# Attention stage in a written order with planned weight steps, first gate tile joined to its fill

## The chip, the cores and the metric

The kernel runs on one core of a Trainium2 chip. The metric is the device time of one execution in microseconds; the time of a kernel is the median over its runs. The core has five engines with instruction queues of their own: TensorE (PE; its weight loads are listed apart as PEld), VectorE (DVE), ScalarE (ACT), GpSimd (POOL) and SyncE (SP), which here only issues DMA transfers. Each engine works through its own instructions in order and waits on semaphores for the others.

## The reference

One layer of a hybrid decoder, T = 1024 positions, width D = 1024, all in float32:

```python
h = rms_norm(x, norm_mix_pre)
q, k, v, cb, cc, cx, g_att, g_conv = split(h @ w_in)       # 6 parts of 512 columns, 2 of 1024
# stick-breaking attention, 8 heads of 64, strictly causal, t = query, s = key:
z = (q . k) / sqrt(64)
A[t, s] = sigmoid(z[t, s]) * prod(1 - sigmoid(z[t, j]) for s < j < t)
o = A @ v
y_att  = o @ w_att_branch
y_conv = (cb * causal_dwconv3(cc * cx)) @ w_conv_branch
m = sigmoid(g_att) * y_att + sigmoid(g_conv) * y_conv
x = x + rms_norm(m @ w_out, norm_mix_post)
h = rms_norm(x, norm_ffn_pre)
a, g = split(causal_dwconv3(h @ w_up))                     # 2 x 2816 columns
x = x + rms_norm((gelu(g) * a) @ w_down, norm_ffn_post)
```

## The kernel before

**Products.** A float32 factor is held as two fp16 halves, high and low, and a product is three passes of fp16 matmuls, `PASSES = ((0, 0), (0, 1), (1, 0))`. One 128 x 512 output of depth 1024 is thus 24 matmuls, and a projection tile of 128 columns for all 1024 positions 48.

**A weight tile and its scale.** Before a weight tile (128 x 1024, 512 KB) can be used it is fetched by a DMA that SyncE issues (`wfetch`), its squares are summed per partition on ScalarE (`sumsq`), and `scale_of` turns the sum into a power of two: VectorE casts the 128 partial sums to bf16 (`rb`, L69 to L71), TensorE adds them over the partitions with a matmul against ones (`pr`, L74), and three tiny VectorE operations on the bits of the sum give the scale and its inverse (L76 to L79). Then `split` writes the high half on ScalarE (L86) and the low half on VectorE (L87). `prep(name)` does this for weights in the order of the list `wseq`, some tiles ahead of the one that is asked for. The sums `pr` are numbered in that order; in the stage they share three PSUM banks (`pm`) with the outputs of the fill.

**The attention stage.** Heads are taken in four pairs j. For a pair, `units_of()` gives six units of up to 512 keys by two query tiles of 128, so there are 24 units and 48 query tiles; the tile `0_1_00` below is pair 0, p = 1, first key 0, second of the unit's two tiles. `stage1` handles one query tile: the scores `z` on TensorE (L455, and a mask matmul); two sigmoids on ScalarE, `R` (of -z, L464) and `be` (of z, L465); two scans along the keys on VectorE, one per head, which turn `R` into running products from right to left (L468); the weights `be` times the shifted `R` (L473); their high half by a ScalarE copy (L476) and low half by a VectorE subtraction (L477), both written over `R`; and a DMA transpose of both into `wT` that SyncE issues. `stage3` multiplies a unit's `wT` with v into `o` (L502), two units behind.

**The fill.** Between these pieces the kernel interleaves independent work for TensorE, as generators with one step per few matmuls: `v_tile` 4 to 7, for each pair `qk_tile` of the next pair's q and k and `conv_tile` (three projections `cc`, `cx`, `cb` and the gated convolution, result `pf`), then `p_split` (the scale of all four `pf` and their split to `p16`), and `branch(0, d)` for d = 0 to 7, the products of the convolution branch with the weights `wc0` to `wc3`, two d per weight. `merge` advances the fill in proportion to the attention's matmuls.

**What sets the order.** The kernel is written with the Tile framework. Its scheduler orders the instructions of each engine from the program order, dependences, priorities and its own model of durations. `stage1` and `stage3` run at high priority, and `stage3` is held behind a given matmul (`tc.issue_after`). So the written place of a fill step is not its place on an engine.

**Behind the stage.** `branches(0, 1, 2)` are the first three products `ywa` = o x `wa` (one weight for two of them). Then `blocks(q)` prepares sums and differences of blocks of `hT`, the normalised input in fp16 halves: the tiles `T1` to `T4` and the operand `hB` on VectorE (L601 and on). `gates(0)` computes the gate tile 0 (`gc0` and `ga0`, 48 matmuls each, sigmoids into two `xp` tiles), `pair_fetch`, `pair_sums` and `pair_split` prepare the weights of gate pair `g1`, and `merge_m(0)` forms the merged tile 0. The gate pairs `g1` to `g7` follow; their first products read `hB` and the split `g1` weights.

Of the kernel before, what the change touches and what calls it, by code (L numbers as in the profile page):

```python
# [24 lines left out]
P = 128  # L25
# [8 lines left out]
KH = KD // 2  # L34
PASSES = ((0, 0), (0, 1), (1, 0))


class Layer:
# [19 lines left out]
    def scale_of(self, sm, n, keep=False, slack=0):  # L58

        nc = self.nc  # L60
        if keep:
            r = self.const.tile([P, 4], F32, tag=f"sc{self.nsc}", name=f"sc{self.nsc}", bufs=1)
        else:
            r = self.smp.tile([P, 4], F32, tag="sc", name=f"sc{self.nsc}", bufs=16)
        self.nsc += 1
        rb = self.smp.tile([P, 1], BF16, tag="rb", name=f"rb{self.nsc}", bufs=8)
        if n > 1:
            nc.vector.tensor_reduce(r[:, 0:1], sm[:, 0:n], AX.X, ALU.add)
            nc.vector.tensor_copy(rb, r[:, 0:1])  # L69
        else:  # L70
            nc.vector.tensor_copy(rb, sm[:, 0:1])  # L71
        pool, shape, tag = self.sum_psum
        ps = pool.tile(shape, F32, tag=tag, name=f"pr{self.nsc}")
        nc.tensor.matmul(ps[:, 0:1], self.ones, rb, start=True, stop=True)  # L74
        ri = r.bitcast(I32)
# [85 lines left out]

    def rstd_of(self, src, name):
# [46 lines left out]
    def build(self):  # L209
# [8 lines left out]
        for j in range(4):  # L218
            if j < 3:
                nt("q", j + 1), nt("k", j + 1)  # L220
            nt("cc", j), nt("cx", j), nt("cb", j)
        for i in range(4):
# [3 lines left out]
        nt("gc", 0), nt("ga", 0)  # L226
# [44 lines left out]
    def mixer(self, mid):  # L271
        tc, nc, a = self.tc, self.nc, self.a
        hT = self.hp.tile([P, 2, KD, T], F16, tag="hT", name="hT")
        with ExitStack() as ph1:
# [74 lines left out]
            def qk_tile(j, which):  # L349
                w, inv = self.prep(f"{which}{j}")  # L350
# [17 lines left out]
                yield  # L368

            def conv_tile(j):  # L370
# [3 lines left out]
                for n, which in enumerate(("cc", "cx", "cb")):  # L374
                    w, inv = self.prep(f"{which}{j}")
# [65 lines left out]
            def stage1(u, tt, tl):  # L441
# [4 lines left out]
                nb = W // P  # L446
                z = pat.tile([P, 2, NH], F32, tag="z", name=f"z{nm}", bufs=2)
                for n, (hq, hk) in enumerate(PASSES):
                    for h in range(2):
                        d = ds(64 * h, 64)  # L450
                        m = nc.tensor.matmul(z[:, h, :W], s["q"][d, hq, ds(i * P, P)], s["k"][d, hk, ds(lo, W)],
                                             start=n == 0, stop=n == 2 and not u["top"], skip_group_check=True)
                if u["top"]:
                    for h in range(2):
                        m = nc.tensor.matmul(z[:, h, W - P:W], self.identb, self.maskb, start=False, stop=True,  # L455
                                             skip_group_check=True)
                u["last"] = m
                R = att.tile([P, 2, NH + 1], F32, tag="R", name=f"R{nm}", bufs=4)
                be = att.tile([P, 2, NH], F32, tag="be", name=f"be{nm}", bufs=2)
                if u["top"]:  # L460
# [3 lines left out]
                nc.scalar.activation(R[:, :, :W], z[:, :, :W], AF.Sigmoid, scale=s["cz"][1])  # L464
                nc.scalar.activation(be[:, :, :W], z[:, :, :W], AF.Sigmoid, scale=s["cz"][0])  # L465
# [4 lines left out]
                if not u["end"]:  # L470
                    carry[tl] = self.smp.tile([P, 2, 1], F32, tag="cy", name=f"cy{nm}", bufs=4)
                    nc.vector.tensor_copy(carry[tl], R[:, :, 0:1])
                nc.vector.tensor_tensor(be[:, :, :W], be[:, :, :W], R[:, :, 1:W + 1], ALU.mult)  # L473
                w = R.rearrange("p h s -> p (h s)").bitcast(F16)[:, :4 * W]
                wv = [w[:, ds(2 * W * hl, 2 * W)].rearrange("p (h s) -> p h s", h=2) for hl in range(2)]
                nc.scalar.activation(wv[0], be[:, :, :W], AF.Copy)  # L476
                nc.vector.tensor_tensor(wv[1], be[:, :, :W], wv[0], ALU.subtract)  # L477
                nc.sync.dma_start_transpose(u["wT"][:, ds(tl * 4 * u["nb"], 4 * nb), :], w)
# [4 lines left out]
            def stage3(u, after):  # L483
# [7 lines left out]
                with tc.issue_after(after):  # L491
                    for q, (hw, hv) in enumerate(((1, 0), (0, 0), (0, 1))):
                        for b in range(NB):
                            sb = lo // P + b
                            both = sb <= 2 * p
                            nb0 = min(NB, 2 * p + 1 - lo // P)
                            for h in range(2):
                                k0, k1 = (2 * hw + h) * nb0 + b, (2 * hw + h) * NB + b + 4 * NB
                                rhs = u["wT"][:, k0:k1 + 1:k1 - k0, :] if both else u["wT"][:, k1, :]
                                out = o[64 * h:64 * h + 64, n0:n0 + 2 * P] if both else \  # L500
                                    o[64 * h:64 * h + 64, n0 + P:n0 + 2 * P]
                                nc.tensor.matmul(out, v16[sb // 2][:, sb % 2, j, 1 + h if hv else 3 * h, :], rhs,  # L502
                                                 start=first and q == 0 and b == 0, stop=q == 2 and b == NB - 1,
                                                 skip_group_check=True)
# [10 lines left out]

            def attention():
                us = list(units_of())
                lag = 2
                for k in range(len(us) + lag):
                    if k < len(us):  # L520
                        u = us[k]
                        while "cz" not in stk.get(u["j"], {}):
                            yield 0
                        u["wT"] = att.tile([P, 32, P], F16, tag="wT", name=f"wT{u['nm']}", bufs=2)
                        for tl in (1, 0):
                            with tc.high_priority():
                                stage1(u, 2 * u["p"] + tl, tl)
                            yield u["nb"]
                    if k >= lag:
                        with tc.high_priority():  # L530
                            stage3(us[k - lag], us[min(k, len(us) - 1)]["last"].ins)
                        yield u["nb"] if k < len(us) else 4

            def chain(*gens):
                for g in gens:
                    yield from g

            def merge(main, n_main, fill, n_fill):

                done, seen, more = 0, 0, True  # L540
                for k in main:
                    seen += k
                    want = seen * n_fill // n_main if k else done + 1
                    while done < want and more:
                        more = next(fill, "end") != "end"
                        done += 1
                assert not more or next(fill, "end") == "end" or True
                for _ in fill:
                    pass

            for which in "qk":
                for _ in qk_tile(0, which):
                    pass
            gens = [v_tile(tt) for tt in range(4, 8)]
            for j in range(4):
                if j < 3:
                    gens += [qk_tile(j + 1, "q"), qk_tile(j + 1, "k")]
                gens.append(conv_tile(j))
            gens += [p_split()] + [branch(0, d, pm) for d in range(8)]
            merge(attention(), 4 * 3 * (2 + 4 + 2 + 4 + 4 + 4), chain(*gens), 32 + 3 * 34 + 4 * 49 + 1 + 64)  # L560

# [8 lines left out]
        with ExitStack() as ph2:  # L570
            sig = {}

            def gates(d):
                for bi, which in enumerate(("gc", "ga")):
                    w, inv = self.prep(f"{which}{d}")
                    sc = sgn[:, 8 + 8 * bi + d:9 + 8 * bi + d]
                    self.mul(sc, inv_h, inv)
                    s = self.xp.tile([P, T], F32, tag="x", name=f"s{which}{d}")
                    for c in range(2):
                        ps = pm.tile([P, NH], F32, tag="pm", name=f"p{which}{d}_{c}")  # L580
                        for _ in self.cm_half(w[0], hT, ps, c):
                            pass
                        nc.scalar.activation(s[:, ds(c * NH, NH)], ps, AF.Sigmoid, scale=sc)
                    sig[which, d] = s


# [47 lines left out]
            branches(0, 1, 2)  # L634
# [5 lines left out]
            gates(0)  # L640
# [7 lines left out]
            ms = [merge_m(0)]  # L648
# [483 lines left out]
```

## Time and profile before

| | |
|---|---|
| median of 3 runs | 1386.92 us (1383.72 to 1388.22) |
| the profiled execution | 1389.26 us |
| its span (first to last instruction) | 1387.5 us |
| mean granted clock of TensorE | 0.978 of full speed |
| busy: TensorE, VectorE, ScalarE, GpSimd | 94%, 72%, 58%, 3% of the span |

The span is divided roughly into the head (norm, first projections) up to 73 us, the attention stage up to 451 us, the gate pairs and the output projection, and the feed-forward network. A row of groups of the profile reads: line, engine, operation, output <- inputs by the program's names, shape, count | busy time in all in us, mean ns of one | idle time of the engine just before them and what ended it. A row of the timeline reads: start in us, length in us, engine, line, operation, names and shape, count, and in brackets the wait ahead of it in us and who ended it. A row of waits reads: who waited <- for whom: time in all, number of times, longest.

### The profile page before, as it was taken

What the parts mean: (1) busy time and instruction counts of PE and PEld (TensorE: products, weight loads), DVE (VectorE), ACT (ScalarE), POOL (GpSimd) and SP (SyncE); (2) the same over time, 40 slices, a digit from 0 to 9 for tenths busy, and PEclk for the clock granted to TensorE, in tenths of its full rate; (3) what the DMA queues carried; (4) which work ended last, traced back from release to release, by engine and by line L of the source; (5) the groups of instructions that cost most, each with busy time, mean ns of one, the idle gap of its engine ahead of it and who ended that gap; (6) DMA issues with size and microseconds to landing.
All of it is one profiled execution on the core that took longest, in us unless ns stands there. A gap on an engine that the chain in (4) does not pass through costs nothing. (4 is left out here: it accounts for less than half of the span.)

```text
span 1387.5 us, 17025 instructions
## 1 busy us (share of the span) xinstructions
PE 1299.4 (94%) x6543; PEld 598.0 (43%) x6543; DVE 1004.6 (72%) x1649; ACT 804.7 (58%) x1138; POOL 48.2 (3%) x69
## 2 busy tenths in 40 slices
PE   5998879888889999999999999999999999999997
PEld 3443434333434444444454444444444444444443
DVE  5669695857741797878688876963882893598848
ACT  6665655546536465775466576664765765576522
POOL 1000000000000000000110000010001001000001
PEclk9999999999999999999999999999999999999999
DMA  7235442534511001251341135156127318712115
GB/s 259 77 65 103 96 95 66 106 81 90 109 46 47 31 32 60 92 182 46 107 140 43 61 114 190 46 131 158 61 90 123 122 61 186 223 61 107 61 61 197
DMA packets 109394, 139.60 MB, mean 101 GB/s; under 512 B 79088, under 2 KB 79088, under 8 KB 109312
## 3 DMA queue, kind: packets, MB, share of 16 engines
q1 hardware_dynamic: 105360, 124.28, 29.6%
q0 software_dynamic: 3952, 14.23, 5.6%
q8 instruction: 51, 0.84, 0.2%
q14 instruction: 31, 0.25, 0.1%
HBM read 94.45 MB, written 25.17 MB: 86 GB/s over the span
## 5 line engine op out<-in xcount | busy, mean ns | idle before, releaser
L1002 PEld LDWEIGHTS <-wh_u 128*128 128x128 f16 x1848 | 178.7, 98 | 217.7 <-issue 4.0
L897 PE MATMUL pd<-wdh,f 128*128 128x512 f16 x1056 | 233.9, 383 | 10.2 <-DVE wdh L87 5.6
L897 PEld LDWEIGHTS <-f 128*128 128x128 f16 x1056 | 104.0, 99 | 138.5 <-issue 14.3
L76 DVE TENSOR_SCALAR sc<-pr 128x1 int32<-128x1 int32 x75 | 10.8, 152 | 110.0 <-PE pr L74 109.9
L1002 PEld LDWEIGHTS <-wh_g 128*128 128x128 f16 x588 | 56.8, 98 | 70.6 <-ACT wh_g L86 2.3
L712 PE MATMUL py<-wh_wo,m 128*128 128x512 f16 x384 | 83.9, 379 | 0.0
L901 ACT ACTIVATE y<-pd,sd 128x512 f32<-128x512 f32 x64 | 42.3, 693 | 63.2 <-PE pd L897 56.9
L87 DVE SCALAR_TENSOR_TENSOR wh_u<-ws_u,sc,wh_u 128x1024 f16<-128x1024 f32 (+1 forms) x66 | 72.1, 1100 | 8.9 <-ACT wh_u L86 8.9
L86 ACT ACTIVATE wh_u<-ws_u,sc 128x1024 f16<-128x1024 f32 (+1 forms) x66 | 64.2, 998 | 22.6 <-DVE ws_u L837 12.6
L476 ACT ACTIVATE R<-be 128x1024 f16<-128x1024 f32 (+3 forms) x48 | 39.2, 839 | 51.3 <-DVE be L473 39.4
L1079 DVE SCALAR_TENSOR_TENSOR ugu<-cgu,cw_g,ugu 128x1023 f32<-128x1023 f32 (+1 forms) x44 | 56.3, 1279 | 9.7 <-ACT ugu L1077 9.5
L203 PE MATMUL pq<-hT,wh_q 128*128 128x512 f16 x192 | 50.3, 422 | 13.1 <-DVE pf L394 11.0
L468 DVE TENSOR_TENSOR_SCAN R<-R,zero 128x256 f32<-128x256 f32 (+3 forms) x64 | 47.9, 804 | 16.1 <-ACT R L464 10.8
L1079 DVE SCALAR_TENSOR_TENSOR ua<-cau,cw_a,ua 128x1023 f32<-128x1023 f32 (+1 forms) x44 | 56.2, 1278 | 2.0 <-ACT ua L1077 1.8
L712 PEld LDWEIGHTS <-m 128*128 128x128 f16 x384 | 37.5, 98 | 44.1
L465 ACT ACTIVATE be<-z,cz 128x1024 f32<-128x1024 f32 (+3 forms) x48 | 42.4, 903 | 23.0 <-DVE R L477 14.5
L502 PE MATMUL o<-wT,v 128*64 128x256 f16 x480 | 31.0, 281 | 25.2 <-DVE o L511 12.7
L464 ACT ACTIVATE R<-z,cz 128x1024 f32<-128x1024 f32 (+3 forms) x48 | 41.7, 894 | 16.1 <-PE z L455 13.2
L203 PE MATMUL pk<-hT,wh_k 128*128 128x512 f16 x192 | 45.5, 395 | 4.6 <-DVE R L461 4.3
L307 PE MATMUL pv<-wh_v,hT 128*128 128x512 f16 x192 | 45.3, 392 | 3.1 <-ACT wh_v L86 1.7
L56 ACT ACTIVATE jk_u<-ws_u 128x1024 bf16<-128x1024 f32 x44 | 46.4, 1055 | 2.6 <-DMA ws_u<-w_up_nt 1.9
L203 PE MATMUL pcx<-hT,wh_cx 128*128 128x512 f16 x192 | 46.0, 388 | 0.0
(606 smaller groups left out, 2543.7 us busy)
## 6 DMA issues: line engine op xcount, KB each, us to landing
ws_u<-w_up_nt SPq DMA_DIRECT2D x44, 512.0 KB, 3.5
yd<-y POOLq DMA_DIRECT2D x24, 512.0 KB, 5.3
ds<-w_down SPq DMA_DIRECT2D x22, 512.0 KB, 6.2
wd<-w_down SPq DMA_DIRECT2D x22, 512.0 KB, 3.5
ws_g<-w_in_nt SPq DMA_DIRECT2D x14, 512.0 KB, 3.5
x<-x SPq DMA_DIRECT2D x8, 512.0 KB, 8.8
ws_wo<-w_out SPq DMA_DIRECT2D x8, 512.0 KB, 6.7
xr<-x SPq DMA_DIRECT2D x8, 512.0 KB, 4.0
```

What stands on the lines that cost most here:

```text
L56: self.nc.scalar.activation(self.junk(f"jk_{name}"), src, AF.Square, accum_out=acc)
L86: self.nc.scalar.activation(dst[:, 0, :], src, AF.Copy, scale=s)
L87: self.nc.vector.scalar_tensor_tensor(dst[:, 1, :], src, s, dst[:, 0, :], ALU.mult, ALU.subtract)
L203: nc.tensor.matmul(ps, w[:, wi, ds(k * P, P)], hT[:, hi, k, ds(c * NH, NH)], start=n == 0, stop=n == last)
L307: nc.tensor.matmul(pv, hT[:, hi, k, ds(tt * P, P)], wv[k // 2][:, wi, ds((k % 2) * NH, NH)], start=n == 0, stop=n == 3 * KD - 1)
L465: nc.scalar.activation(be[:, :, :W], z[:, :, :W], AF.Sigmoid, scale=s["cz"][0])
L468: nc.vector.tensor_tensor_scan(rev, rev, self.zero.broadcast_to([P, W]), 2.0 ** 14 if u["top"] else carry[tl][:, h, :], ALU.mult, ALU.add)
L712: nc.tensor.matmul(ps, m16[k][:, hi, ds(tt * P, P)], wo[k][:, wi, sl], start=k == 0 and p == 0, stop=k == 7 and p == 2)
L897: nc.tensor.matmul(ps, f16[g][k][:, hi, ds(tt * P, P)], w[k][:, wi, sl], start=n == 0, stop=n == 3 * GROUPS[g] - 1)
L901: nc.scalar.activation(y[:, sl], ps, AF.Copy, scale=sm[:, 0:1])
L1002: nc.tensor.matmul(ps, w[wt][:, wi, ds(wc * NH + k * P, P)], self.block(i, hi, k), start=first and n == 0, stop=n == 3 * KH - 1, skip_grou ...
L1079: nc.vector.scalar_tensor_tensor(u[:, lag:], c[:, :T - lag], sm[:, 2 - lag:3 - lag], u[:, lag:], ALU.mult, ALU.add)
```

## The change

It is one change in four parts.

1. **Written order.** From `qk_tile(0)` to the end of `attention()` the program runs under `tc.manual_schedule` for TensorE, ScalarE, VectorE and SyncE: on these engines each instruction keeps the place that it has in the program. GpSimd is still placed by the scheduler. `high_priority` and `issue_after` go.
2. **One query tile at a time.** `stage1` is cut into `scores` (TensorE and the two sigmoids), `scan`, `weigh`, and `turn` in two parts (the ScalarE copy; the VectorE subtraction and the transpose). The loop over tiles takes them in the order: scores of this tile, copy of the last tile, scans of this tile, subtraction and transpose of the last tile, weigh of this tile; after a unit's second tile the products of the unit two back; and then a stretch of fill steps, by the share of attention matmuls done.
3. **Planned weights.** A weight of the fill is no longer prepared by `prep` where it is used. `scale_of` is cut into `scale_sum` (the cast `rb` and the matmul `pr`) and `scale_pow` (the three tiny operations). `plan_weight` enters five actions for each weight into a table `steps`, by fill step: fetch 46 steps ahead of the use, squares 36, sum 30, scale and high half 25, low half 21, each with an earliest step. `plan_p` does the same for the sum and split of `pf`. A fill step holds 3 matmuls in most generators, and its planned actions run ahead of it.
4. **Fill and tail.** The gate tile 0 becomes two generators `gate0` in the fill, its sigmoids held in two `slab` tiles, and `branch(0, 4)` to `branch(0, 7)` leave the fill: they run right behind the stage, under the scheduler again. The four weights `wa0` to `wa3` are still prepared by `prep`, behind the stage. `gates(0)` goes from its old place, and `merge_m(0)` comes ahead of `branches(1, 2)`.

Two places show how instructions move. The first is the sum `pr5` of the weight `k1`, where the stage begins. On VectorE (`x6`, `x7`: the last norms; `v16`: evictions of v; `sc`: the tiny scale operations), before:

```order
L170 TENSOR_SCALAR r_pre7_421<-r_pre7_421 128x1
L292 SCALAR_TENSOR_TENSOR x6_338<-x6_338,r_pre6_404,g_pre_118 128x1024
L292 SCALAR_TENSOR_TENSOR x7_385<-x7_385,r_pre7_421,g_pre_118 128x1024
L71 CAST rb4_552<-sm_q1_471 128x1
L316 SCALAR_TENSOR_TENSOR v16_1_112<-pv3_357,v16_1_112 128x4x64 x2
L76 TENSOR_SCALAR sc2_460<-pr3_463 128x1
L71 CAST rb5_563<-sm_k1_476 128x1
L78 TENSOR_SCALAR sc2_460<-sc2_460 128x1
```

and after:

```order
L526 MEMSET R0_1_00_737 128x2
L531 SCALAR_TENSOR_TENSOR R0_1_00_737<-R0_1_00_737,zero_102 128x384 x2
L550 TENSOR_TENSOR R0_1_01_667<-be0_1_01_668,R0_1_01_667 128x1024
L540 TENSOR_TENSOR be0_1_00_738<-be0_1_00_738,R0_1_00_737 128x2x384
L197 SCALAR_TENSOR_TENSOR wh_q1_713<-ws_q1_588,sc3_691,wh_q1_713 128x1024
L76 CAST rb5_751<-sm_k1_614 128x1
L86 TENSOR_SCALAR sc4_750<-pr5_753 128x1
```

The cast of `k1` stood among the operations ahead of the stage; now it stands behind the scans (the L531 row), the subtraction (L550) and the weigh (L540) of a query tile and the low half of `q1`. On TensorE, before:

```order
L190 MATMUL pt_pre7_427<-ident_80,x7_385 128x128 x8
L203 LDWEIGHTS wh_q0_0_457
L203 MATMUL pq0_1_524<-hT_104,wh_q0_0_457 128x512
L74 LDWEIGHTS ones_85
L74 MATMUL pr4_554<-rb4_552,ones_85 128x1
L74 LDWEIGHTS ones_85
L74 MATMUL pr5_565<-rb5_563,ones_85 128x1
L203 LDWEIGHTS wh_q0_0_457
```

and after:

```order
L510 MATMUL z0_1_00_728<-k0_528,q0_473 128x384
L514 LDWEIGHTS identb_95
L514 MATMUL z0_1_00_728<-maskb_97,identb_95 128x128
L514 LDWEIGHTS identb_95
L514 MATMUL z0_1_00_728<-maskb_97,identb_95 128x128
L79 LDWEIGHTS ones_85
L79 MATMUL pr5_753<-rb5_751,ones_85 128x1
L346 LDWEIGHTS hT_104
```

The sum stood within the projection of q0; now it comes directly behind the scores of the same query tile whose scans stand ahead of its cast on VectorE.

The second place is behind the stage. On TensorE, at the last matmul of `ywa3`, before:

```order
L422 LDWEIGHTS wh_wa1_0_3523
L422 MATMUL pywa3_1_4092<-o16_3_3455,wh_wa1_0_3523 128x512
L203 LDWEIGHTS wh_gc0_0_3919
L203 MATMUL pgc0_0_4110<-hT_104,wh_gc0_0_3919 128x512
L203 LDWEIGHTS wh_gc0_0_3919
```

and after:

```order
L482 LDWEIGHTS wh_wa1_0_4054
L482 MATMUL pywa3_1_4206<-o16_3_3324,wh_wa1_0_4054 128x512
L79 LDWEIGHTS ones_85
L79 MATMUL pr33_4234<-rb33_4231,ones_85 128x1
L482 LDWEIGHTS wh_wa2_0_4065
L482 MATMUL pywa4_0_4263<-o16_0_985,wh_wa2_0_4065 128x512
```

The gate products no longer stand between `ywa3` and `ywa4`; a sum (`pr33`, for the pair `g1`) does. At the start of the `wa` products, after:

```order
L482 LDWEIGHTS wh_wc3_3774
L482 MATMUL pywc7_1_3964<-p16_3_3558,wh_wc3_3774 128x512
L79 LDWEIGHTS ones_85
L79 MATMUL pr29_3988<-rb29_3986,ones_85 128x1
L482 LDWEIGHTS wh_wa0_0_3993
L482 MATMUL pywa0_0_4013<-o16_0_985,wh_wa0_0_3993 128x512
```

so the sum of `wa0` comes right ahead of its first use. On VectorE, around the start of `T1`, before:

```order
L429 TENSOR_SCALAR ywa2_3997<-pywa2_0_3998,sgn_446 128x512
L601 TENSOR_TENSOR T1_0_4037<-hT_104 128x1024
L87 SCALAR_TENSOR_TENSOR wh_ga0_0_3993<-ws_ga0_0_3781,sc31_3985,wh_ga0_0_3993 128x1024
L603 TENSOR_TENSOR T1_0_4037<-T1_0_4037,hT_104 128x1024
L429 TENSOR_SCALAR ywa2_3997<-pywa2_1_4012,sgn_446 128x512
```

and after:

```order
L489 TENSOR_SCALAR ywa1_4079<-pywa1_1_4094,sgn_446 128x512
L489 TENSOR_SCALAR ywa2_4111<-pywa2_0_4112,sgn_446 128x512
L677 TENSOR_TENSOR T1_0_4151<-hT_104 128x1024
L679 TENSOR_TENSOR T1_0_4151<-T1_0_4151,hT_104 128x1024
L489 TENSOR_SCALAR ywa2_4111<-pywa2_1_4126,sgn_446 128x512
```

Both times `T1` begins behind the first eviction of `ywa2`.

The diff, cut to its core:

```diff
+ENGINES = {mybir.EngineType.PE, mybir.EngineType.Activation, mybir.EngineType.DVE, mybir.EngineType.SP}
...
+    def plan_weight(self, steps, name, at):
...
+        def fetch():
+            h["sm"] = self.small(f"sm_{name}", w=8)
+            h["t"] = self.ws.tile([P, D], F32, tag="ws", name=f"ws_{name}")
+            nc.sync.dma_start(h["t"], src)
+        def squares():
+            self.sumsq(h["t"], h["sm"][:, 0:1], name)
+        def total():
+            h["r"], h["ps"] = self.scale_sum(h["sm"], 1)
+        def split():
+            h["s"], inv = self.scale_pow(h["r"], h["ps"])
+            w = self.wh.tile([P, 2, D], F16, tag="wh", name=f"wh_{name}")
+            nc.scalar.activation(w[:, 0, :], h["t"], AF.Copy, scale=h["s"])
+            self.wdone[name] = [w], inv
+        def low():
+            w = self.wdone[name][0][0]
+            nc.vector.scalar_tensor_tensor(w[:, 1, :], h["t"], h["s"], w[:, 0, :], ALU.mult, ALU.subtract)
+        for f, lead, floor in ((fetch, 46, -1), (squares, 36, 5), (total, 30, 11), (split, 25, 15), (low, 21, 18)):
+            steps.setdefault(max(floor, at - lead), []).append(f)
...
+                for f, q in [(total, 5), (power, 10)] + [(part(j), 12 + 4 * j) for j in range(4)]:
+                    steps.setdefault(at + q, []).append(f)
...
+            fill = ([(v_tile(tt), 8, None) for tt in range(4, 8)])
+            for j in range(4):
+                if j < 3:
+                    fill += [(qk_tile(j + 1, w), 16, f"{w}{j + 1}") for w in "qk"]
+                fill.append((conv_tile(j), 48, (f"cc{j}", f"cx{j}", f"cb{j}")))
+            fill += [(gate0("gc", 0), 16, "gc0"), (gate0("ga", 1), 16, "ga0")]
+            fill += [(branch(0, d, pm), 8, f"wc{d // 2}" if d % 2 == 0 else None) for d in range(4)]
...
+            def run_fill(upto):
+                while state["done"] < upto:
+                    for f in steps.pop(state["done"], ()):
+                        f()
+                    next(chained, None)
+                    state["done"] += 1
...
-                        for tl in (1, 0):
-                            with tc.high_priority():
-                                stage1(u, 2 * u["p"] + tl, tl)
-                            yield u["nb"]
-                    if k >= lag:
-                        with tc.high_priority():
-                            stage3(us[k - lag], us[min(k, len(us) - 1)]["last"].ins)
...
+                for k in range(len(us) + 2):
+                    for tl in (1, 0):
+                        if k < len(us):
+                            u = us[k]
+                            t = scores(u, 2 * u["p"] + tl, tl)
+                            seen += 3 * (t["W"] // P) + 1
+                        else:
+                            t = None
+                        if last is not None:
+                            turn(last, 0)
+                        if t is not None:
+                            scan(t)
+                        if last is not None:
+                            turn(last, 1)
+                        if t is not None:
+                            weigh(t)
+                        last = t
+                        if tl == 0 and k >= 2:
+                            products(us[k - 2])
+                        run_fill(seen * (n_fill - 24) // total + 6 * max(0, 2 * (k - len(us)) + 2 - tl))
...
-            merge(attention(), 4 * 3 * (2 + 4 + 2 + 4 + 4 + 4), chain(*gens), 32 + 3 * 34 + 4 * 49 + 1 + 64)
+            self.prep("q0", 1)
+            with tc.manual_schedule(engines=ENGINES):
+                for which in "qk":
+                    for _ in qk_tile(0, which):
+                        pass
+                attention()
+            self.wpos = self.fpos = len(self.wseq) - 4
...
-            branches(0, 1, 2)
+            for d in range(4, 8):
+                for _ in branch(0, d, pm):
+                    pass
+            branches(0)
+            ms = [merge_m(0)]
+            branches(1, 2)
...
             branches(3)
-            gates(0)
...
             branches(4, 5)
             self.pair_sums("g2")
-            ms = [merge_m(0)]
```

More of the change, by code (lines that the diff above doesn't have):

```diff
@@ L58, in scale_of, with scale_sum @@
     def scale_of(self, sm, n, keep=False, slack=0):
+        return self.scale_pow(*self.scale_sum(sm, n, keep), slack)
+    def scale_sum(self, sm, n, keep=False):
         nc = self.nc
@@ L490, in stage3 @@
                 n0 = (2 * p - 4 * c) * P
[L491 to L504, printed above, removed]
+                for q, (hw, hv) in enumerate(((1, 0), (0, 0), (0, 1))):
+                    for b in range(NB):
+                        sb = lo // P + b
+                        both = sb <= 2 * p
+                        nb0 = min(NB, 2 * p + 1 - lo // P)
+                        for h in range(2):
+                            k0, k1 = (2 * hw + h) * nb0 + b, (2 * hw + h) * NB + b + 4 * NB
+                            rhs = u["wT"][:, k0:k1 + 1:k1 - k0, :] if both else u["wT"][:, k1, :]
+                            out = o[64 * h:64 * h + 64, n0:n0 + 2 * P] if both else \
+                                o[64 * h:64 * h + 64, n0 + P:n0 + 2 * P]
+                            nc.tensor.matmul(out, v16[sb // 2][:, sb % 2, j, 1 + h if hv else 3 * h, :], rhs,
+                                             start=first and q == 0 and b == 0, stop=q == 2 and b == NB - 1,
+                                             skip_group_check=True)
                 if p % 2 == 1 and u["end"]:
@@ new lines, in mixer @@
+            steps, n_fill = {}, 0
+            for g, n, names in fill:
+                if names == "gc0":
+                    plan_p(steps, n_fill)
+                for e, name in enumerate((names,) if isinstance(names, str) else names or ()):
+                    self.plan_weight(steps, name, n_fill + 16 * e)
+                n_fill += n
+            for e in (2, 3):
+                self.plan_weight(steps, f"wc{e}", n_fill + 16 * (e - 2))
+            chained = (q for g, _, _ in fill for q in g)
@@ L534, in chain @@
[L534 to L559, printed above, removed]
-            merge(attention(), 4 * 3 * (2 + 4 + 2 + 4 + 4 + 4), chain(*gens), 32 + 3 * 34 + 4 * 49 + 1 + 64)
+                total = sum(3 * u["nb"] + 1 + (3 * min(u["nb"], 2 * u["p"] + 1 - u["lo"] // P) + 1) for u in us)
@@ new lines, in attention @@
+                seen, last = 0, None
+                for f in steps.pop(-1, ()):
+                    f()
+                for k in range(len(us) + 2):
[4 more added lines that the diff above has]
+                            seen += 3 * (t["W"] // P) + 1
+                        else:
+                            t = None
[11 more added lines that the diff above has]
+                        run_fill(seen * (n_fill - 24) // total + 6 * max(0, 2 * (k - len(us)) + 2 - tl))
@@ L570, in mixer @@
         with ExitStack() as ph2:
[L571 to L584, printed above, removed]
             hB = self.h7p.tile([P, 2, 3, KH, NH], F16, tag="hB", name="hB")
```

98 lines of the change are left out of this document (60 added, 38 removed).

## Prediction

> **What bounds the kernel now.** I read the page, then the stretches of the attention stage, then what TensorE waited for, then TensorE and VectorE in order of time around the stage's end.
>
> ```profile
> span 1387.5 us, 17025 instructions
> PE 1299.4 (94%) x6543; PEld 598.0 (43%) x6543; DVE 1004.6 (72%) x1649; ACT 804.7 (58%) x1138; POOL 48.2 (3%) x69
> ```
>
> TensorE is the bound; 88 us of the span are idle. The stage from the first scores (72.8) to the first `wa` product (450.7), then the 64 us behind it:
>
> ```profile
> 72.80:450.70 377.90, 332.19 (x2010) 153.74 (x2010) 254.10 (x448) 213.74 (x289) 0.00 (x0) 0.94 0.38 83
> 450.70:515.00 64.30, 62.93 (x293) 28.26 (x293) 55.81 (x75) 31.61 (x44) 0.00 (x0) 1.00 0.07 25
> ```
>
> The first number is the length, then the busy time of PE, PEld, DVE and ACT; 0.94 is the clock. TensorE idles 377.90 - 332.19 = 45.7 us in the stage and works at 0.94 clock. Behind it TensorE is full, and VectorE busy for 55.8 of 64.3. The waits:
>
> ```profile
> PE o L502 <- DVE o L511: 12.7, 5, 4.2
> PE o L502 <- DMA wT<-R: 12.3, 7, 5.0
> PE pq L203 <- DVE pf L394: 11.0, 2, 5.5
> ...
> PE pr L74 <- DVE rb L71: 2.5, 1, 2.5
> ```
>
> Note the last: TensorE's sum over partitions (`pr`) waits for VectorE's cast (`rb`) once, 2.5 us. The scheduler put casts and sums where their inputs were ready.
>
> A gap also costs clock:
>
> ```profile
> 99.55 2.04 PE L502 MATMUL o<-wT,v 128*64 128x256 f16 x24 [2.65 <-DMA wT<-R]
> ...
> 147.76 1.50 PE L502 MATMUL o<-wT,v 128*64 128x256 f16 x24
> ...
> 201.16 12.82 PE L203 MATMUL pq<-hT,wh_q 128*128 128x512 f16 x48 [5.50 <-DVE pf L394]
> ...
> 281.84 13.43 PE L203 MATMUL pq<-hT,wh_q 128*128 128x512 f16 x48 [5.51 <-DVE pf L394]
> ...
> 323.49 0.69 PE L502 MATMUL o<-wT,v 128*64 128x256 f16 x12 [2.39 <-DVE o L511]
> ...
> 380.56 10.52 PE L203 MATMUL pcx<-hT,wh_cx 128*128 128x512 f16 x48
> ...
> 390.95 10.52 PE L203 MATMUL pcb<-hT,wh_cb 128*128 128x512 f16 x48
> ```
>
> 48 matmuls take 10.4 us (start to start of the 380.56 and 390.95 rows: 0.216 each; the rows show 10.52 with the last one's end), but 2.3 to 2.9 more behind a gap of 5.5. After 2.39 nothing is lost, after 2.65 half a microsecond in the first 24. I take 2.2 us per gap from 2.5 up, near the 48-matmul rows because most new gaps are longer than 2.65; bounds 0.5 and 2.9. Eight gaps or close pairs of that size lie in the stage: 17.6 us, below the 0.06 x 378 = 23 that the clock column allows.
>
> **The change, term by term.** Fill and attention keep their matmuls: `gc0`/`ga0` (96) come into the stage, `wc` 4 to 7 (96) go out, to right behind it, so the work on TensorE stays as it is. Two things that move cost nothing that I count: the weights of `q1` to `cx0` are prepared inside the stage and no longer ahead of it, where TensorE was fed all the same, and the sigmoids of gate 0 take two `slab` tiles for two of `xp`. Removed: the scheduler's waits, -45.7 at most, and their clock, -17.6. I take all of it: products stand two units behind, `o` is read long before it is reused, and each tile's VectorE work is spread over its own fill. Bound: the 12.3 for `wT` stays.
>
> Added: TensorE, VectorE, ScalarE and SyncE now keep the written order, and all fill steps come behind `weigh(t)`. So a weight's cast stands on VectorE behind both scans of the tile, `turn` of the last tile and `weigh`; its `pr` stands among TensorE's fill. Behind the waiting `pr` queue the rest of the fill and the next tile's scores, and for those wait ScalarE's next sigmoids and VectorE's next scans, so a pause is not worked off elsewhere. The scans cannot start before this tile's scores and `R` sigmoid. Durations:
>
> ```profile
> L468 DVE TENSOR_TENSOR_SCAN R<-R,cy,zero 128x512 f32<-128x512 f32 x32 | 39.3, 1268 | 0.3
> L468 DVE TENSOR_TENSOR_SCAN R<-R,zero 128x384 f32<-128x384 f32 x16 | 14.3, 935 | 0.0
> L473 DVE TENSOR_TENSOR be<-be,R 128x1024 f32<-128x1024 f32 x24 | 29.2, 1216 | 0.4
> L473 DVE TENSOR_TENSOR be<-be,R 128x768 f32<-128x768 f32 x8 | 7.6, 950 | 0.0
> L477 DVE TENSOR_TENSOR R<-be,R 128x1024 f16<-128x1024 f32 x24 | 29.2, 1216 | 0.8 <-ACT R L476 0.8
> L464 ACT ACTIVATE R<-z,cz 128x768 f32<-128x768 f32 x8 | 7.1, 892 | 0.0
> 405.75 4.87 DVE L87 SCALAR_TENSOR_TENSOR p<-pf,sc,p 128x1024 f16<-128x1024 f32 x4 [0.54 <-ACT p L86]
> ```
>
> The last row shows that neighbours overlap: four of 1.28 in 4.87, so 1.2 each; I take 0.07 off each row. `pr5` (sum of `k1`): TensorE reaches it 0.7 us after tile `0_1_00` starts, right behind its scores. The cast is ready after scores 0.7, `R` 0.9 plus 0.1, scans 2 x 0.87, `turn` 1.14, `weigh` 0.88, the split of `q1` that stands ahead of it 1.2 and 0.2 for itself: 6.9. Stall 6.2. Worked so, by the matmuls between scores and sum, for pr4 to pr28: 4.1, 6.2, 4.8, 2.7, 3.4, 3.5, 5.3, 1.0, 2.7, 5.2, 4.7, 3.9, 2.1, 1.8, 4.5, 1.7, 5.1, 2.2, 3.0, 6.6, 1.5, 5.0, 2.4, 2.2, 0: 25 stalls, 85.6 us. Sixteen are 2.5 or longer: 16 x 2.2 = 35.2 of slow clock. Bounds: each chain 1 us shorter (no overlap lost, `turn` early) gives 61.6 and 12 gaps; each 0.3 longer gives 93.
>
> Beside other work: the weights' splits and squares are the same instructions as before, hidden by 254 of VectorE and 214 of ScalarE in 378; if that cover went, VectorE would lag and lengthen the chains (0 to 6 us, not added). PSUM has three banks, so a late eviction can hold a fill group; the new pauses make room (0 to 10, not added). On SyncE's queue each weight fetch now stands behind the transposes:
>
> ```profile
> ws_cc<-w_in_nt SPq DMA_DIRECT2D x3, 512.0 KB, 3.5
> wT<-R SPq DMA_TRANSPOSE x48, 4.3
> ```
>
> A fetch leads its squares by ten steps, 30 matmuls, 6.5 us, against 3.5: nothing, and 3.5 per late weight if not. GpSimd's queue is passed by nothing that waits.
>
> Behind the stage. The `gc0`/`ga0` products no longer stand between `wa` 0-3 and `wa` 4. The rows: TensorE and VectorE in order of time, then a group of this stretch and one of the stage.
>
> ```profile
> 450.73 10.52 PE L422 MATMUL pywa<-o,wh_wa 128*128 128x512 f16 x48
> ...
> 471.47 10.52 PE L203 MATMUL pgc<-hT,wh_gc 128*128 128x512 f16 x48
> 481.83 10.52 PE L203 MATMUL pga<-hT,wh_ga 128*128 128x512 f16 x48
> ...
> 513.07 2.32 PE L1002 MATMUL pg1b<-hB,wh_g 128*128 128x512 f16 x10
> ```
>
> ```profile
> 463.90 0.75 DVE L429 TENSOR_SCALAR ywa<-pywa,sgn 128x512 f32<-128x512 f32 x1 [1.35 <-PE pywa L422]
> ...
> 465.70 1.28 DVE L87 SCALAR_TENSOR_TENSOR wh_ga<-ws_ga,sc,wh_ga 128x1024 f16<-128x1024 f32 x1
> ...
> 509.42 1.28 DVE L87 SCALAR_TENSOR_TENSOR wh_g<-s_g,sc,wh_g 128x1024 f16<-128x1024 f32 x1
> ```
>
> ```profile
> L623 DVE TENSOR_TENSOR ywc<-ywc,sgc 128x1024 f32<-128x1024 f32 x1 | 1.2, 1218 | 0.0
> ```
>
> ```profile
> L86 ACT ACTIVATE wh_wa<-ws_wa,sc 128x1024 f16<-128x1024 f32 x4 | 4.5, 1136 | 0.0
> ```
>
> VectorE's chain from the eviction of `ywa2` (463.90) to the split of `s12` (510.70) is 46.8 us long and ended 2.4 before TensorE needed it. The gates gave 20.7 of that cover. In the new order VectorE still starts `T1` only behind the eviction of `ywa2`, so the 20.7 of `wc` 4-7 ahead of it cover nothing. The chain is shorter by one split (1.2) and three merge operations (3 x 1.14): 42.2. From the end of `wc7`: the sum of `wa0` now stands right ahead of its use, wait 0.5 + 1.14 + 0.5 = 2.1; 60 matmuls (13.0) to `ywa2`, so the chain ends at 57.4. TensorE is there after 2.1 + 144 matmuls (31.1) + 24 (5.2) + 21 (4.6) = 43.0. Stall 57.4 - 43.0 = 14.4, clock 2.2; with 2.1, 18.7. Bounds of the stall: 8.4 if the scheduler puts five of the chain's 1.2-us operations behind the split, 16.8 if the 2.4 by which it ended early are not to be had.
>
> Sum against the profiled execution, 1389.3 us (1387.5 span and 1.8 around it): 1389.3 - 45.7 - 17.6 + 85.6 + 35.2 + 18.7 = 1465.5. It lies 2.3 above the median of the runs, so I predict 1463.
>
> The Trainium skill, "TensorE: Matmul & The Clock Gate", Part 1, says that the clock halves after an idle window of about 3.4 us and comes back after about as long of work. By it only the 13 stalls from 3.4 up would pay, 1.7 each: an estimate of 22 for the 35.2, and 1452 for the sum. The 99.55 row, slow behind 2.65, does not fit the sharp limit, so the rows decide.
>
> **Rivals.**
> - Faster: the casts come in time and only the gains are left. For it: one wait of 2.5 for a cast in the whole stage today, and VectorE idle for a third of it. Against: the cast's place in the new order, which nothing on VectorE may overtake. With the stalls gone: 1387 - 63.3 + 18.7 = 1342; with 10 us of bank waits 1352. It decides below (63.3 - 18.7)/25 = 1.8 us per sum, clock included; I find 3.4 without it.
> - The stalls come, but the clock stays up, since the work between is dense: 1463 - 35 = 1428. For it the 323.49 row, against it the 99.55 row.
> - The chain behind the stage is hidden, because the scheduler's VectorE runs ahead: 1463 - 16.6 = 1446. Against it: 55.8 busy of 64.3.
> - The change does nothing in the stage, pauses merely moving from one wait to another: about 1387 + 18.7 = 1406.
>
> **How the numbers follow.** Forecast 0.58, clock stays up 0.17, chain hidden 0.08, nothing in the stage 0.08, faster 0.09. The forecast's own range is 1424 (short chains -24, four gaps fewer -9, the stall behind the stage at 8, -6) to 1498 (long chains 7, VectorE's lag 6, bank waits 10, clock at 2.9 a gap, 11). The range takes in the second and third rival and reaches to the fourth: 1408 to 1500. Faster by over 0.3% (4 us, about what a measurement of this kernel tells from no change) 0.09, within 0.02, slower 0.89.
>
> **What would show it.** In the profile after: about 25 TensorE waits for `rb` of some 85 us, 3.4 each; the other three waits above gone or small; a clock near 0.90 in the stage; 435 us from the first scores to the first `wc4` product (377.9 - 63.3 + 120.8); VectorE below 62% busy in it; behind it one wait of some 14 us for the `g1` weights or their sum, with VectorE full. Wrong it would be if VectorE's casts stand ahead of the tile's scans in time, if evictions hold TensorE instead, or if the pauses shrink to 1 or 2 us.

## The result

The changed kernel takes 1489.56 us (median of 4 runs, 1487.92 to 1490.64) against 1385.85 for the kernel before on the same chip: 1.0747 times as long, 95% interval 1.0724 to 1.0770. The forecast was 1463 in a range of 1408 to 1500. The head of its page:

```profile
span 1488.5 us, 16951 instructions
PE 1330.4 (89%) x6543; PEld 600.0 (40%) x6543; DVE 1007.1 (68%) x1649; ACT 804.4 (54%) x1138; POOL 48.1 (3%) x69
```

The span is 101.0 longer for the same number of matmuls. TensorE is idle 158 us in place of 88, and its busy time is 31 longer for the same work, mostly by the slow clock. The stretches: the stage from the first scores to the first `wc4` product, then `wc` 4 to 7 and the wait for `wa0`, then the rest behind:

```profile
71.99:527.74 455.75, 357.36 (x2010) 154.36 (x2010) 260.96 (x469) 209.85 (x284) 0.00 (x0) 0.88 0.32 71
527.74:553.98 26.24, 21.05 (x98) 9.41 (x97) 0.87 (x7) 14.62 (x24) 0.00 (x0) 1.00 0.03 13
553.98:640.00 86.02, 71.27 (x302) 30.74 (x303) 77.09 (x112) 46.84 (x65) 0.00 (x0) 0.88 0.19 56
```

The stage took 377.90 before and takes 455.75, at a clock of 0.88 for 0.94: 77.9 longer. From there to the end it was 936.8 (1387.5 - 450.7) and is 960.8 (1488.5 - 527.74): 24.0 longer. The scores begin 0.8 earlier. Together 101.1.

All waits of TensorE from the first scores to the stage's last `o` product (522.70):

```profile
PE pr L79 <- DVE rb L76: 92.6, 23, 7.8
PE pr L79 <- DVE rb L74: 5.0, 1, 5.0
```

These are the 24 stalls at the sums, 97.6 us; L74 is the cast of the `pf` sum. The waits for `o`, for `wT` and for `pf`, which headed this list in the kernel before, are gone. One stall in order of time, that of `pr5`, all engines (rows of weight loads, the fetch and gaps of other work left out):

```profile
91.45 0.66 PE L510 MATMUL z<-k,q 64*128 64x384 f16 x6
...
92.36 0.90 ACT L518 ACTIVATE R<-z,cz 128x768 f32<-128x768 f32 x1 [1.51 <-PE z L514]
...
93.30 1.81 DVE L531 TENSOR_TENSOR_SCAN R<-R,zero 128x384 f32<-128x384 f32 x2 [1.65 <-ACT R L518]
...
95.03 1.23 DVE L550 TENSOR_TENSOR R<-be,R 128x1024 f16<-128x1024 f32 x1
96.17 0.95 DVE L540 TENSOR_TENSOR be<-be,R 128x768 f32<-128x768 f32 x1
97.05 1.28 DVE L197 SCALAR_TENSOR_TENSOR wh_q<-ws_q,sc,wh_q 128x1024 f16<-128x1024 f32 x1
...
98.24 0.15 DVE L76 CAST rb<-sm_k 128x1 bf16<-128x1 f32 x1
98.44 0.16 PE L79 MATMUL pr<-rb,ones 128*128 128x1 bf16 x1 [6.12 <-DVE rb L76]
98.44 0.13 PEld L346 LDWEIGHTS <-hT 128*128 128x128 f16 x2 [6.24 <-issue]
98.47 5.72 PE L346 MATMUL pv<-wh_v,hT 128*128 128x512 f16 x15
```

Scores, sigmoid, scans, subtraction, weigh, split, cast, sum: the chain of the prediction, with a stall of 6.12 where it had 6.2. Then 15 matmuls take 5.72. Fifteen of the same form took 3.40 at the start of the stage, where no gap was ahead:

```profile
72.54 3.40 PE L346 MATMUL pv<-wh_v,hT 128*128 128x512 f16 x15
```

### The profile page after: what moved, and what is told of

Its sections match the earlier page's. It is cut to its first block, busy times and chain, and to the rows that moved or that the text cites. A ratio compares the mean times of both kernels' runs of the same rounds, so it can differ in the third digit from the quotient of the medians.

```text
span 1488.5 us, 16951 instructions
## 1 busy us (share of the span) xinstructions
PE 1330.4 (89%) x6543; PEld 600.0 (40%) x6543; DVE 1007.1 (68%) x1649; ACT 804.4 (54%) x1138; POOL 48.1 (3%) x69
## 5 line engine op out<-in xcount | busy, mean ns | idle before, releaser
L976 PE MATMUL pd<-wdh,f 128*128 128x512 f16 x1056 | 232.2, 381 | 10.3 <-DVE wdh L97 5.7
L79 PE MATMUL pr<-rb,ones 128*128 128x1 bf16 x75 | 11.9, 167 | 118.4 <-DVE rb L76 95.9
L531 DVE TENSOR_TENSOR_SCAN R<-R,zero 128x256 f32<-128x256 f32 (+3 forms) x64 | 49.3, 811 | 68.0 <-ACT R L518 67.9
L96 ACT ACTIVATE wh_u<-ws_u,sc 128x1024 f16<-128x1024 f32 (+1 forms) x66 | 64.2, 998 | 22.6 <-DVE ws_u L916 12.6
L531 DVE TENSOR_TENSOR_SCAN R<-R,cy,zero 128x512 f32<-128x512 f32 x32 | 39.4, 1272 | 40.0 <-ACT R L518 39.7
L1158 DVE SCALAR_TENSOR_TENSOR ugu<-cgu,cw_g,ugu 128x1023 f32<-128x1023 f32 (+1 forms) x44 | 56.3, 1280 | 10.1 <-ACT ugu L1156 10.0
L242 PE MATMUL pcb<-hT,wh_cb 128*128 128x512 f16 x192 | 52.0, 429 | 0.0
L346 PE MATMUL pv<-wh_v,hT 128*128 128x512 f16 x192 | 48.8, 411 | 2.4 <-ACT wh_v L96 1.7
L242 PE MATMUL pcx<-hT,wh_cx 128*128 128x512 f16 x192 | 50.6, 420 | 0.0
L242 PE MATMUL pcc<-hT,wh_cc 128*128 128x512 f16 x192 | 50.2, 420 | 0.0
L482 PE MATMUL pywa<-o,wh_wa 128*128 128x512 f16 x192 | 48.5, 416 | 1.9 <-ACT wh_wa L96 1.9
```

The lines of the kernel that those rows point to most:

```text
L96: self.nc.scalar.activation(dst[:, 0, :], src, AF.Copy, scale=s)
L242: nc.tensor.matmul(ps, w[:, wi, ds(k * P, P)], hT[:, hi, k, ds(c * NH, NH)], start=n == 0, stop=n == last)
L346: nc.tensor.matmul(pv, hT[:, hi, k, ds(tt * P, P)], wv[k // 2][:, wi, ds((k % 2) * NH, NH)], start=n == 0, stop=n == 3 * KD - 1)
L482: nc.tensor.matmul(ps, w[0][:, wi, ds((d % 2) * NH + k * P, P)], acts[bi][k][:, hi, ds(c * NH, NH)], start=n == 0, stop=n == 11)
L531: nc.vector.tensor_tensor_scan(rev, rev, self.zero.broadcast_to([P, W]), 2.0 ** 14 if u["top"] else carry[tl][:, h, :], ALU.mult, ALU.add)
L976: nc.tensor.matmul(ps, f16[g][k][:, hi, ds(tt * P, P)], w[k][:, wi, sl], start=n == 0, stop=n == 3 * GROUPS[g] - 1)
```

## The experiments

A stretch below runs from the first scores to the last `o` product, and its columns are those of the tables above. For the changed kernel it is

```profile
71.99:522.70 450.71, 353.09 (x1992) 152.58 (x1991) 259.08 (x467) 207.86 (x280) 0.00 (x0) 0.88 0.32 72
```

My theory was the prediction's: a cast that stands on VectorE behind its own tile, with its sum in TensorE's order, stalls TensorE; the gaps cost clock; behind the stage VectorE's chain lost its cover.

**Control: fetch and squares earlier.**

```diff
-        ... (fetch, 46, -1), (squares, 36, 5), (total, 30, 11), ...
+        ... (fetch, 56, -1), (squares, 46, 5), (total, 30, 11), ...
```

> Control: fetch and squares of every planned weight ten fill steps earlier (56 and 46 ahead of the use), cast and sum where they are. Theory (the cast is late because it stands on VectorE behind the scans, subtraction and weigh of its own query tile): nothing changes, 1485 to 1494 us, about 24 waits of TensorE for the cast of 95 to 100 us in the stage. Rival (the squares on ScalarE or the fetch are late and hold the cast): the waits shrink, by up to all 98 us, and the time falls below 1460.

Measured 1492.37 us, with 24 waits at the sums of 96.5 us together. The casts did not wait for squares or transfers.

**Cast ahead of the scans.** `scale_sum` is cut into cast and matmul; before `scan(t)` the loop issues the casts of the sums that this tile's fill will hold. Squares as in the control.

```diff
+                        upto = seen * (n_fill - 24) // total + 6 * max(0, 2 * (k - len(us)) + 2 - tl)
+                        for q in range(state["done"], upto):
+                            for f in early.pop(q, ()):
+                                f()
                         if t is not None:
                             scan(t)
...
```

> As the control, and the cast of each weight is written ahead of the scans of the tile whose fill holds its sum; the sum keeps its place on TensorE. Theory: the cast no longer waits for this tile's scores, sigmoid and scans; of the 97.6 us of stalls in the stage at most 10 to 30 stay (a cast behind the last tile's evictions), and with the gaps goes their slow clock, 42 us in the stage: 1489.6 - 97.6 - 42 + 20 = 1370, 1345 to 1395. Rival (the pauses move to another wait, since VectorE's chain per tile sets the pace): 1440 to 1490. Rival of the squares: as the control, no further gain.

Measured 1382.95 us, 0.9967 of the kernel before (0.9954 to 0.9980), and 109 below the control, from which it differs in nothing but the casts' place. The stretch falls to 341.6, and the waits in it are

```profile
PE pr L83 <- DVE rb L76: 10.4, 6, 3.8
PE pr L83 <- DVE rb L74: 10.3, 1, 10.3
PE pcc L250 <- DVE k L407: 1.6, 2, 1.3
```

The 23 stalls of 92.6 us fell to 6 of 10.4. The second row is the `pf` sum, which was left in its place; its wait grew from 5.0 to 10.3 (why stays open), and small waits of 3.3 in all are new (the third row is one of them). So the pauses moved to other waits only in small part.

**Sum later.** The cast stays, the matmul goes into the fill of a later tile, with the scale and both halves behind it (and `wc2` and `wc3` are planned six steps closer together, so that they fit).

```diff
+        ... (cast, 30, 11), (total, 20, 18), (split, 15, 20), (low, 11, 22)
```

> Cast where it is (30 steps ahead), but the sum on TensorE 20 ahead, in the fill of a later tile, the scale and high half 15, the low half 11 (wc2 and wc3 six to twelve steps earlier). Theory: the cast is done a whole tile before its sum, so all stalls but that of the pf sum go: 1489.6 - 92.6 - 40 = 1357, 1340 to 1375, and faster than the kernel before. Rival (pace set by VectorE's chain): TensorE waits for evictions or wT in place of the casts, 1440 to 1490. Rival (later splits come too late for their first use): new waits for the weight's halves, 1400 and more.

Measured 1370.50 us, 0.9886 (0.9860 to 0.9913). In the stretch one wait for a cast is left besides the `pf` sum's 9.9, of 0.3 us; other waits are 5.3 together. Moving the cast up or the sum down mends the same thing, so it is their distance that counts, and the written order as such is no hindrance.

**Gaps filled.** The changed kernel with matmuls that nobody reads ahead of the 20 sums that waited 2.3 us or longer.

```diff
+        for _ in range(self.busy.get(self.nsc, 0)):
+            nc.tensor.matmul(ps, self.hT0[:, 0:P], self.hT0, start=True, stop=True)
         nc.tensor.matmul(ps[:, 0:1], self.ones, rb, start=True, stop=True)
```

> The changed kernel with matmuls that nobody reads ahead of the 20 sums that waited 2.3 us or longer, as many as fill the gap but 0.6 us (360 in all, 77.8 us at full clock). Stalls keep their length, TensorE is not idle in them. Theory (idle gaps cost clock behind them, 2.1 us for each from 2.3 up): the waits shrink to some 20 us, the clock in the stage rises from 0.88 to 0.97 or more, and the time falls by 35 to 42 us to 1448 to 1455. Rival (the slow stretches are not caused by the gaps): time as before or longer, 1489 to 1500, clock below 0.92.

Measured 1450.88 us, 38.7 less than without them. The stretch, and `pr5` again in order of time on TensorE:

```profile
70.61:482.40 411.79, 392.03 (x2352) 178.70 (x2351) 259.09 (x467) 207.69 (x280) 0.00 (x0) 1.00 0.37 79
```

```profile
89.09 5.56 PE L80 MATMUL pr<-hT 128*128 128x512 f16 x25
95.37 0.16 PE L81 MATMUL pr<-rb,ones 128*128 128x1 bf16 x1 [0.72 <-DVE rb L76]
95.40 4.69 PE L350 MATMUL pv<-wh_v,hT 128*128 128x512 f16 x21
```

TensorE gets 360 matmuls more (77.8 us at 0.216) and the stretch is 38.9 us shorter. Without them the busy time is 392.0 - 77.8 = 314.2, against 353.1: the slow clock of the stage was 38.9, and all of it came from the gaps. Behind the filled gap 21 matmuls run at full speed.

**The scheduler again.** The changed program with the manual schedule left out, and nothing else.

```diff
-            with tc.manual_schedule(engines=ENGINES):
+            with ExitStack():
```

> The changed kernel without the manual schedule: the same program text, planned steps, cut tiles, gates in the fill, but the scheduler orders all engines. Theory (the fixed order of casts and sums makes the loss in the stage): the scheduler moves casts forward, few waits for casts stay, the stage takes 370 to 400 us as before; with the tail's 24: 1387 + 24 = 1411, 1390 to 1425. Rival (the planned steps or the tile-wise form cost by themselves): above 1450.

Measured 1360.25 us, 0.9811 (0.9783 to 0.9838): better than the kernel before, and 50 better than I expected. The stretch, and TensorE and VectorE at `pr4`:

```profile
70.08:391.40 321.32, 314.29 (x1990) 143.67 (x1991) 261.70 (x460) 201.68 (x272) 0.00 (x0) 0.99 0.45 99
```

```profile
78.63 2.34 DVE L531 TENSOR_TENSOR_SCAN R<-R,zero 128x512 f32<-128x512 f32 x2 [0.55 <-ACT R L518]
79.22 0.17 PE L79 MATMUL pr<-rb,ones 128*128 128x1 bf16 x1
```

The sum runs while the same tile's scans do: the scheduler had put the cast ahead of them. So in the stage the planned steps, the cut tiles and the gates in the fill cost nothing; they gain. From the first scores to the first `wa` product it is now 352.6 us (70.08 to 422.7), with 96 gate matmuls (20.7 us) that the kernel before did later; that one needed 377.9 without them, so the gain there is 46; which of the three makes it, no run separates. My expectation had missed it by taking the stage's time from the kernel before. Behind the first `wa` product the scheduler does not help: from there to the end it is 936.6 us (1359.3 - 422.7), and the kernel before took 936.8 with the 20.7 of the gates in it. So the text behind the stage loses some 20 us, whichever way the stage is ordered; its sum of `g1` waits 9.2 here, 9.45 in the changed kernel.

**Blocks early.** The changed kernel with the VectorE chain ahead of `wc` 4 to 7.

```diff
+            for q in range(2):
+                blocks(q)
             for d in range(4, 8):
                 for _ in branch(0, d, pm):
                     pass
...
-            for q in range(2):
-                blocks(q)
             branches(3)
```

> The changed kernel with blocks(0) and blocks(1) written ahead of the wc 4 to 7 products, so that VectorE's T and hB chain lies beside them; the stage is untouched. Theory (behind the stage the chain starts too late for want of the gate products' cover): the waits of 9.4 for the sum of g1, 4.1 and 1.2 behind it and the slow clock of the two long ones, 4, go: 1489.6 - 19 = 1471, 1468 to 1478. Rival (the sum of g1 waits for its fetch or squares, not for the chain): within 3 us of 1489.6.

Measured 1481.79 us, a gain of 7.8 where 19 were expected. TensorE and the cast of `wa0` in order of time, first in the changed kernel, then here, then with `wa0` prepared ahead of the blocks (the next run):

```profile
551.95 0.16 PE L79 MATMUL pr<-rb,ones 128*128 128x1 bf16 x1 [3.33 <-DVE rb L76]
553.98 1.89 PE L482 MATMUL pywa<-o,wh_wa 128*128 128x512 f16 x4 [1.87 <-ACT wh_wa L96]
...
585.94 0.16 PE L79 MATMUL pr<-rb,ones 128*128 128x1 bf16 x1 [9.45 <-DVE rb L74]
...
602.94 2.75 PE L1081 MATMUL pg1a<-hT,wh_g 128*128 128x512 f16 x12 [1.24 <-ACT cgg L1096]
609.76 0.16 PE L79 MATMUL pr<-rb,ones 128*128 128x1 bf16 x1 [4.07 <-DVE rb L74]
```

```profile
559.93 0.16 DVE L76 CAST rb<-sm_wa 128x1 bf16<-128x1 f32 x1 [2.17 <-ACT jk_wa L57]
...
560.13 0.16 PE L79 MATMUL pr<-rb,ones 128*128 128x1 bf16 x1 [13.42 <-DVE rb L76]
...
585.73 0.16 PE L79 MATMUL pr<-rb,ones 128*128 128x1 bf16 x1 [0.96 <-DVE rb L74]
```

```profile
549.31 0.16 PE L79 MATMUL pr<-rb,ones 128*128 128x1 bf16 x1 [0.41 <-ACT ywc L487]
549.89 20.88 PE L482 MATMUL pywa<-o,wh_wa 128*128 128x512 f16 x96 [0.41 <-ACT ywc L487]
572.41 0.16 PE L79 MATMUL pr<-rb,ones 128*128 128x1 bf16 x1 [1.64 <-DVE rb L74]
```

The stalls at the sums of `g1` and `g2` and between them, 14.8 us, did go to 1.0, but the cast and the squares of `wa0` now queued behind the chain, and that sum waited 13.4 in place of 3.3. In the changed kernel VectorE was idle there, and its cast waited for the squares of `wa0`, which ScalarE did behind the last `ywc` work:

```profile
551.74 0.16 DVE L76 CAST rb<-sm_wa 128x1 bf16<-128x1 f32 x1 [26.21 <-ACT jk_wa L57]
```

So the late squares make the 3.33 us, and the high half of `wa0`, which can only follow the sum, the 1.87 behind it.

**Blocks early, wa0 ahead of them.** One line more, `self.prep("wa0")` ahead of the blocks.

> The changed kernel with the blocks ahead of wc 4 to 7, and ahead of these the weight wa0 prepared. Theory (with the blocks alone the gain went into the sum of wa0, whose cast and squares then queued behind the chain, 13.4 us in place of 3.3): now that wait goes as well, 1481.8 - 13.4 - 1.9 - 2 = 1464, 1460 to 1469. Rival (the chain's operations hold TensorE in another place whatever stands ahead): 1476 to 1485.

Measured 1466.97 us: 22.6 below the changed kernel, of the 24.0 lost behind the stage. So this loss is shown too. The sum of `wa0`, now ahead of the `wc` products, still waits 3.6.

**Put together.** First the later sums and the early blocks:

> Sums ten steps later (as in the run of 1370.5) and the blocks ahead of wc 4 to 7. Theory, the two losses are separate and add: 1370.5 - 19 = 1352, 1347 to 1358. Rival (VectorE has no room for the chain beside a stage's end without stalls): above 1362.

Measured 1360.42 us, a gain of 10.1 over the later sums alone, missed for the same reason: the `wa0` sum waits 13.7. Then also `wa0` ahead of the blocks, and the cast of the `pf` sum nine steps ahead of its matmul:

> As e7, the weight wa0 prepared ahead of wc 4 to 7, and the cast of the pf sum nine steps ahead of its matmul. Theory: the waits at wa0 (3.3 + 1.9) and for the pf sum (5.0) and their clock (4) go too: 1352 - 14 = 1338, 1333 to 1345. Rival (another wait takes their place, an eviction or the split of pf): 1348 to 1355.

Measured 1344.56 us, 0.9695 (0.9663 to 0.9726), at the upper edge of the range. And the same text with and without the manual schedule, on one chip:

> The text of e8 (sums later, blocks and wa0 early, pf cast ahead) without the manual schedule. Theory (the scheduler finds an order at least as good once the program text is this one; the written order adds nothing): 1340 to 1350, within 0.5% of e8. Rival (the written order itself is worth something once the sums come late): 1355 to 1370.

> e8 once more, on the chip of e9, to compare the two: 1344.6 within 3 us.

Measured 1342.75 us under the scheduler (0.9688, 0.9661 to 0.9715), 1345.46 in the written order (0.9711, 0.9687 to 0.9736). They are 2.7 us (0.2%) apart, every run under the scheduler below every run in the written order. So what wins 3% over the kernel before is the program text; the written order carries it out nearly as well, and adds nothing.

## Why the prediction was right, and where its sizes were off

- **The mechanism** (casts behind their own tile, sums in TensorE's order, 24 or 25 stalls): shown by the two runs that part cast and sum, in opposite ways, with the squares excluded by the control.
- **The removed waits**: taken in full (45.7), and in full they went; the sums excepted, TensorE waited for nothing between the first scores and the last `o` product. So the late fetches and late evictions that the text named and did not add came to nothing there (its three PSUM banks are those of the fill's pool `pm`). Their clock was 17.6 in the sum. The run under the scheduler gives 339.6 busy us up to the first `wa` product at a clock of about 0.99 (314.29, and 25.34 to there); less 20.7 for the gates that is 318.9 for the work on which the kernel before was busy 332.2: 13.3.
- **The stalls: 85.6 forecast, 97.6 measured**, and this term holds the largest miss. Most single ones are near: 4.1, 6.2, 4.8, 2.7 forecast for the first four, 3.82, 6.12, 4.47, 2.50 measured. Eight (`pr8`, `pr9`, `pr10`, `pr15`, `pr17`, `pr20`, `pr23`, `pr27`) ran over by 1.0 to 3.2 and make 12.9; the rest came out 0.9 short. The step that failed is the start of the chain: it let `R` follow the scores at once (0.1) and the scans follow `R`, as if ScalarE and VectorE were free then. Two cases, `pr10` and the 24th stall (`pr27`):

```profile
193.75 1.10 ACT L518 ACTIVATE R<-z,cz 128x1024 f32<-128x1024 f32 x1
193.88 2.60 DVE L420 SCALAR_TENSOR_TENSOR pf<-u,cmw,pf 128x1023 f32<-128x1023 f32 x2 [1.15 <-ACT pf L418]
...
196.41 1.22 DVE L531 TENSOR_TENSOR_SCAN R<-R,zero 128x512 f32<-128x512 f32 x1
...
200.31 0.16 PE L79 MATMUL pr<-rb,ones 128*128 128x1 bf16 x1 [7.18 <-DVE rb L76]
```

```profile
492.56 0.82 PE L510 MATMUL z<-k,q 64*128 64x512 f16 x6
...
495.84 1.04 ACT L57 ACTIVATE jk_wc<-ws_wc 128x1024 bf16<-128x1024 f32 x1
...
496.88 1.10 ACT L518 ACTIVATE R<-z,cz 128x1024 f32<-128x1024 f32 x1
...
502.92 0.19 PE L79 MATMUL pr<-rb,ones 128*128 128x1 bf16 x1 [5.41 <-DVE rb L76]
```

  In the first, the convolution of the last fill stretch holds VectorE until 196.4, though `R` was ready at 194.85: 7.18 for a forecast of 5.3. In the second, ScalarE gets to `R` at 496.88, 3.5 us after the scores' end, since a split, an eviction and squares of the last fill stand ahead: 5.41 for 2.2. The text named VectorE's lag, 0 to 6, but did not add it. In `pr8`, `pr9` and `pr17` too an engine came late to its tile. In `pr15`, `pr20` and `pr23` a convolution stands between `weigh` and the cast, and VectorE waits 1.15 in it for ScalarE's part; that is near the 1.1 to 1.3 by which these three ran over, though the prediction does not show their working.
- **The clock: 35.2 forecast, 38.9 measured** (by the filled gaps). The price per gap, 2.2, was near: worked from sum to sum in the timeline, the 20 gaps of 2.37 and longer lost 1.6 to 2.8 each, 2.1 in the mean. That would be some 42; the run with the filled gaps gives 1.9 each, and I take the difference for the error of this working. Their number was 20 where I had 16. The rival "clock stays up", 0.17, is refuted.
- **Behind the stage: 18.7 forecast, 24.0 measured.** The chain's stall is 14.8 (9.45, 1.24 and 4.07) for 14.4. The sum of `wa0` costs 3.33 + 1.87 = 5.2 for 2.1: I had only the cast, sum and split there, and the squares were late as well. An eviction adds 0.8. The slow clock was 5.7 for 2.2, the largest miss in this term: TensorE is busy 918.8 us from there to the end, for 913.2, since the gaps at `wa0`, `g1` and `g2` all cost clock and I had priced one. Against these 26.5 stand 2.5 us of waits that the kernel before had behind its stage and this one has not.
- Together: idle time of the stage 98.4 - 45.7 = 52.7 (the stalls and 0.8 of others); its busy time, the clock, 357.4 - 332.2 = 25.2, for 17.6 in the forecast; behind it 24.0; the head -0.8. That is 101.1, for the 76.2 of the forecast (1465.5 - 1389.3).
- **The rival "faster"** needed the casts in time. It was priced 1342 to 1352 with the 18.7 behind the stage in it. The run that has them in time and the tail as it was takes 1370.5: the tail cost 24.0, the removed clock was 13.3 and not 17.6, and 15.5 us of waits stay in the stage, 9.9 of them at the `pf` sum. The 1344.6 was reached only with the tail mended and the `pf` cast moved.

## What to carry to other kernels

When the order of an engine is written by hand, a tiny operation between two engines (here a cast of one column for a matmul of one column) takes the whole latency of what is written ahead of it: give producer and consumer different tiles in the text. Before putting work ahead of a wait, look for what else queues behind that work: the chain that was moved early took 14.8 us of waits away and made another grow from 3.3 to 13.4. To learn whether an order or the program text is at fault, let the scheduler order the same text: one line showed that the text of the stage was a gain of 46 us in the scheduler's order, and that the loss behind the stage was not the order's.

## What the runs showed of the hardware

In the stage of the changed kernel the clock falls behind slightly shorter gaps than I expected, and the price depends little on the gap's length. TensorE behind gaps of 1.87, 2.38 and 5.66 us:

```profile
310.91 0.16 PE L79 MATMUL pr<-rb,ones 128*128 128x1 bf16 x1 [1.87 <-DVE rb L76]
310.93 2.75 PE L242 MATMUL pq<-hT,wh_q 128*128 128x512 f16 x12
...
232.20 0.16 PE L79 MATMUL pr<-rb,ones 128*128 128x1 bf16 x1 [2.38 <-DVE rb L76]
232.22 3.36 PE L242 MATMUL pk<-hT,wh_k 128*128 128x512 f16 x9
...
253.15 0.16 PE L79 MATMUL pr<-rb,ones 128*128 128x1 bf16 x1 [5.66 <-DVE rb L76]
253.17 6.47 PE L242 MATMUL pcc<-hT,wh_cc 128*128 128x512 f16 x21
```

Twelve matmuls behind the first take 2.75, as elsewhere at full clock. Nine behind the second take 3.36 (2.10 at full clock), 21 behind the third 6.47 (4.69). Of the 24 stalls, the four up to 1.87 lost at most 0.4 us, and the four from 2.37 to 2.50 already 1.6 to 1.8. The limit is not sharp: the 323.49 row of the kernel before lost nothing behind 2.39. With longer gaps the price stays: 21 matmuls, as behind the third, took 6.38 behind a gap of 3.82, 7.02 behind 6.12 and 6.87 behind 7.77. The Trainium skill, "TensorE: Matmul & The Clock Gate", Part 1, gives an idle window of about 3.4 us for the fall of the clock; these four gaps and the 38.9 us do not agree with that limit, by which only the 15 gaps from 3.4 up would have paid, an estimate of 25 us at 1.7 each. The estimate of 1.7 a gap that follows from the same window is of the measured size (1.9), a little low.
